# A chunked recurrence inside one decoder block: its small products joined in two stretches a chunk, its decay moved into the next chunk's vectors

## Chip, cores and metric

One core of one Trainium2 chip runs the whole program as one launch. The metric is the device time of that launch in microseconds (us), the median of several runs. The engines are named as in the profile: PE is TensorE (PEld its weight loads), DVE is VectorE, ACT is ScalarE, POOL is GpSimd, SP is SyncE, which here only issues DMAs.

## What is computed

One residual block of a hybrid decoder on 512 tokens of width 1024, all in float32: a norm, one wide input projection, two mixers side by side (a sparse attention and an RWKV-7 recurrence), gates, an output projection, then a gated MLP with a short convolution. The part that matters here is the recurrence: 8 heads, a 64 by 64 state per head, one step for each token.

```python
def step(state, inp):
    r_t, w_t, k_t, v_t, a_t, b_t = inp
    sa = jnp.einsum('bhij,bhj->bhi', state, a_t)
    state = state * w_t[:, :, None, :] + sa[..., None] * b_t[:, :, None, :] + v_t[..., None] * k_t[:, :, None, :]
    return state, jnp.einsum('bhij,bhj->bhi', state, r_t)
...
_, y = lax.scan(step, state0, xs)
...
y = (y - mean) * lax.rsqrt(var + GN_EPS) * ln_g.reshape(H, N) + ln_b.reshape(H, N)
```

`w_t` is the decay, a factor for each channel of the state.

## The kernel before

**The recurrence by chunks.** The 512 tokens are cut into NCH = 8 chunks of C = 64, and the 8 heads stand as 4 pairs (index p) of two (index r). All that does not depend on the state is made ahead of the loop: `AR[:, p, c, 0]` and `AR[:, p, c, 1]` are a chunk's decayed a and r vectors, `BKT` its b and k vectors turned round, `AB` the masked products of these vectors with each other (the part for the state's correction already inverted), `UV` holds the values v and takes up the corrections u, and `PC[:, p, c]` is the decay over the whole of chunk c. The state is the tile `M`, 128 partitions by 256 columns. For chunk c the loop makes these products on PE, each a group of small matrices of 64 by 64:

- X += AR0 · M and Y = AR1 · M, from the state at the chunk's start (32 entries in the trace). X already holds the chunk's own part (`x_own`).
- U = AB · Xs, where `Xs` is X copied to SBUF by DVE, together with `x_own` of the next chunk (32 entries). U is copied into `UV` by ACT and DVE.
- Mp = BKT · UV (16 entries), from which DVE makes the next state in two operations, M1 = (M0 + Mp) * PC, and Y += AB · UV (16 entries), which ACT copies to `Ys`.

Every second chunk `group_norm` normalizes the 128 tokens in `Ys`, on DVE and ACT (`next(gn)`), and then turns them with four transposes on PE beside four small products (`run(gn)`).

**Dense work between them.** These three groups are chained, each waiting for a copy on DVE or ACT of what the one before gave. So the loop calls `next(fill, None)` between them: `fill_chain` is a generator of independent dense work, the rest of the projections and the compression MLP. `dense_fm_g` is one projection of 128 columns, 24 products of 128 by 512 (16 with the high parts `whi`, 8 with the low parts `wlo`), and yields once after the 12th. Weights come by DMA into `raw` (three buffers in turn) from the SP queue; ACT rounds them to `whi`, and DVE (for some POOL) makes `wlo = raw - whi`, one projection ahead.

**What sets the order.** PE and SP take their instructions in the order in which the code writes them (`tc.manual_schedule`). DVE, ACT and POOL are ordered by the framework's scheduler when the program is built, and each then works through its list in order. The products of `kv_proj(1, 280)` and of the compression (`raw,sg` in the trace: 16 products of 128 by 256) come first in the chain. `norm_keys` and `rstd` are short chains on DVE of 8 to 32 columns (`rs_m`, `rs_y`, `kss`, `qss`), after which POOL multiplies the keys and queries (L949, L1008). POOL also issues the DMAs that add up pieces of a later weight (`wsum`).

Of the kernel before, what the change touches and what calls it, by code (L numbers as in the profile page):

```python
# [25 lines left out]
DH = 64  # L26
H = 8
# [56 lines left out]
def hybrid_block(ctx: ExitStack, tc: tile.TileContext, A: dict, out: bass.AP):  # L84
# [28 lines left out]
    def mmb():  # L113
        return bank("mm", 4)

    def pa():
        return bank("a", 2)

    def pb():
        return bank("b", 2)  # L120

    def mm(o, l, r, start, stop):
        te.matmul(o, lhsT=l, rhs=r, start=start, stop=stop)  # L123
# [4 lines left out]
    def act(o, i, f=AF.Copy, **kw):  # L128
        sc.activation(o, i, f, **kw)  # L129

    def tt(o, a, b, op):
        v.tensor_tensor(o, a, b, op=op)  # L132
# [219 lines left out]
    def wsplit_():  # L352
        if loads:
            raw, kt, n, eng = loads.pop(0)
            if eng is None:
                ahead.append(raw)
                return
            if eng == "quarters":
                while len(loads) < len(QUARTER_TILES):
                    wload()  # L360
                ahead.append(first_quarters(raw, *(loads.pop(0)[0] for _ in range(len(QUARTER_TILES) - 1))))
                return
            if type(eng) is tuple:
                eng = eng[1]
                hi, lo = (spare[:, i].rearrange("p (k n) -> p k n", n=n) for i in range(2))
                act(hi, raw)
            else:
                hi = wp.tile([128, kt, n], F32R, name="whi", tag="whi", bufs=2)
                if late:
                    late.pop()(hi, raw)  # L370
                else:
                    act(hi, raw)
                lo = wp.tile([128, kt, n], F32R, name="wlo", tag="wlo", bufs=2)
            ahead.append((hi, lo))
            behind.append(lambda: eng.tensor_tensor(lo, raw, hi.bitcast(F32), op=ALU.subtract))  # L375
            if not hold:
                behind.pop()()

    hold, behind = [], []

    def lows():
        while behind:
# [518 lines left out]
    def heads(ap):  # L901
        return ap.rearrange("p (h d) -> p h d", d=DH)
# [92 lines left out]
    with tc.manual_schedule(engines={mybir.EngineType.PE, mybir.EngineType.Pool, mybir.EngineType.SP}):  # L995
        for m in range(NGA):
            act(siga[m], dense_fm(hh, hl), AF.Tanh, scale=0.5)
        below(0)
        below(16)
        next(fill)  # L1000
        left(0)
        next(fill)
        left(16)
        next(fill)
        norm_keys(0)
        rstd(qss.rearrange("p t h -> p (t h)"), DH)
        for t in range(NT):
            nc.gpsimd.tensor_tensor(heads(qn[:, t]), heads(qn[:, t]), qss[:, t, :, None].to_broadcast([128, 8, DH]),  # L1008
                                    op=ALU.mult)
    dbg("AB", AB)  # L1010
    close(tp_cm)
    kv1 = fill
# [73 lines left out]
        ptv = pt[:, 0:64].rearrange("p (g n) -> p g n", g=2)  # L1086
        act(KC, ptv, AF.Copy, scale=kg)

    def group_norm(c0, Ys):
        n1 = tp.tile([128, H], F32, name="n1", tag="n1", bufs=2)  # L1090
        bc = n1[:, :, None].to_broadcast([128, H, DH])
        v.tensor_reduce(n1, Ys, axis=AX.X, op=ALU.add)
        ts(n1, n1, -1.0 / DH, None)
        tt(Ys, Ys, bc, ALU.add)
        sq = tp.tile([128, H, DH], F32, name="sq", tag="o", bufs=2)
        act(sq, Ys, AF.Square)
        v.tensor_reduce(n1, sq, axis=AX.X, op=ALU.add)
        rstd(n1, DH, 64e-5, "g")
        tt(Ys, Ys, bc, ALU.mult)
        yield  # L1100
        qs = slice(C * c0, C * c0 + 128)
        pt = pa()
        gg = pb()
        o = tp.tile([128, NH2, 128], F32, name="o", tag="o", bufs=2)
        for p in range(NH2):
            ps_ = slice(128 * p, 128 * p + 128)
            te.transpose(pt[:, ps_], Ys[:, 2 * p:2 * p + 2].rearrange("p h d -> p (h d)"), ident)
            mm(gg[:, ps_], g2[:, ps_], sg[:, qs], True, True)
        for p in range(NH2):
            act(o[:, p], pt[:, 128 * p:128 * p + 128], AF.Identity, scale=col("rwkv_ln_g", p),  # L1110
                bias=col("rwkv_ln_b", p))
        tt(o, o, BO[:, :, qs], ALU.add)
        tt(BO[:, :, qs], o, gg.rearrange("p (a t) -> p a t", a=NH2), ALU.mult)
# [26 lines left out]
    def bias_rows(a):  # L1140
        o = 127 - 16 * a
        nc.sync.dma_start(BT[16 * a:16 * a + 16, :, 256:512],
                          vd[:, 0:16 * 384].rearrange("h (i m) -> i h m", m=384)[:, :, o:o + 256])
# [22 lines left out]
    def hsl(r, n=64):  # L1166
        return slice(64 * r, 64 * r + n)
# [8 lines left out]


    with tc.manual_schedule(engines={mybir.EngineType.PE, mybir.EngineType.SP}):
        M0 = Ys = gn = None
        X = pb()  # L1180
        x_own(0, X)
        next(fill, None)
        for c in range(NCH):
            Y = pa()
            if M0 is not None:
                for p in range(NH2):
                    for r in range(2):
                        mm(X[hsl(r), 64 * p:64 * p + 64], AR[hsl(r), p, c, 0, :], M0[hsl(r), p, :], False,
                           p == NH2 - 1)
                    for r in range(2):  # L1190
                        mm(Y[hsl(1 - r), 64 * p:64 * p + 64], AR[hsl(r), p, c, 1, :], M0[hsl(r), p, :], p == 0, False)
            Xs = tp.tile([128, NH2, DH], F32, name="Xs", tag="Xs", bufs=2)
            v.tensor_copy(Xs, X[:, 0:256].rearrange("p (a d) -> p a d", d=DH))
            next(fill, None)
            U = pb()
            if c < NCH - 1:
                X = pb()
            for p in range(NH2):
                for r in range(2):
                    mm(U[hsl(r), 64 * p:64 * p + 64], AB[hsl(r), c, p, r, 0:64], Xs[hsl(r), p], True, True)  # L1200
                if c < NCH - 1:
                    x_own(c + 1, X, (p,))
            act(UV[0:64, c, :, 0, :], U[0:64, 0:256].rearrange("p (a d) -> p a d", d=DH))
            v.tensor_copy(UV[64:128, c, :, 1, :], U[64:128, 0:256].rearrange("p (a d) -> p a d", d=DH))
            next(fill, None)
            if c < NCH - 1:
                Mp = pa()
                for p in range(NH2):
                    for r in range(2):
                        mm(Mp[hsl(r), 64 * p:64 * p + 64], BKT[:, c, p, r, :], UV[:, c, p, r, :], True, True)  # L1210
                M1 = tp.tile([128, NH2, DH], F32, name="M", tag="M", bufs=2)
                mpv = Mp[:, 0:256].rearrange("p (a d) -> p a d", d=DH)
                pc = PC[:, :, c:c + 1].to_broadcast([128, NH2, DH])
                if M0 is None:
                    tt(M1, mpv, pc, ALU.mult)
                else:
                    tt(M1, M0, mpv, ALU.add)
                    tt(M1, M1, pc, ALU.mult)
            for p in range(NH2):
                for r in range(2):  # L1220
                    mm(Y[hsl(1 - r), 64 * p:64 * p + 64], AB[:, c, p, r, 64:128], UV[:, c, p, r, :],
                       M0 is None and p == 0, p == NH2 - 1)
            if c % 2 == 0:
                Ys = tp.tile([128, H, DH], F32, name="Ys", tag="Ys", bufs=2)
            for r in range(2):
                act(Ys[hsl(c % 2), r::2, :], Y[hsl(1 - r), 0:256].rearrange("p (h d) -> p h d", d=DH))
            if c % 2 == 1:
                gn = group_norm(c - 1, Ys)
                if c < NCH - 1:
                    next(gn)  # L1230
            M0 = M1
            if 4 <= c < 6:
                for a in range(4 * c - 16, 4 * c - 12):
                    bias_rows(a)
            if c == NCH - 2:
                bias_compressed()
            if c == NCH - 1:
                for h0 in range(0, H, 4):
                    act(BT[:, h0:h0 + 4, 0:256], BT[:, h0:h0 + 4, 256:257].to_broadcast([128, 4, 256]))
            next(fill, None)  # L1240
            if gn is not None and c % 2 == 0:
                run(gn)
                gn = None
    close(rp_cm)


# [14 lines left out]
    def keys(b):  # L1261
# [7 lines left out]
        for g in range(2):  # L1269
            i, o = slice(64 * g, 64 * g + 64), slice(64 - 64 * g, 128 - 64 * g)  # L1270
            nc.gpsimd.dma_start(KH[o, b, g], KH[i, b, g])
            nc.gpsimd.dma_start(KL[o, b, g], KL[i, b, g])

    def after(inst, other):
        tc.add_manual_dep(inst.ins, other.ins.name, mybir.DependencyInfo(
            mybir.DependencyClass.NoSync, mybir.DependencyReason.DATA), reason="order on one engine")

    def ob_parts(t, behind=None):
        qs = slice(128 * t, 128 * t + 128)
# [786 lines left out]
```

## Time and profile before

| what | value |
|---|---|
| time, median of 3 runs | 790.45 us (790.05 to 791.07) |
| the profiled execution's own time | 790.52 us |
| its span, first to last instruction | 788.8 us |
| PE busy | 782.7 us, 99% of the span |
| DVE busy | 643.1 us, 82% |
| ACT busy | 496.1 us, 63% |
| POOL busy | 110.6 us, 14% |
| the recurrence's loop | about 171 to 270 us of the span |

The span is the time from the first to the last instruction of the profiled execution; 1.7 us of its time lie outside. Busy shares are shares of the span. Products on PE overlap, so a row's duration is longer than the distance to the next row's start; it is the distances between starts that add up.

### The profile page before, as it was taken

The page shows a single profiled execution, that of the slowest core. Times are in us where ns is not written, and L with a number is a line of the kernel's source. Part 1 is how long each engine was busy: PE and PEld are TensorE (multiplying, and loading weights), DVE is VectorE, ACT ScalarE, POOL GpSimd, SP SyncE. Part 2 cuts the span into 40 slices and gives each one's busy share as a digit, 9 for nine tenths or more (in the row PEclk, how much of TensorE's full clock was granted, in tenths as well). Part 3 has the DMA queues.
Part 4 walks back from the last instruction along what each step waited for, and adds up shares of the span by engine and source line. Part 5 has one row for each costly group of instructions (what it writes and reads, how often), then busy time and mean ns, then how long its engine had stood idle before and what let it go on. Part 6 is the DMA issues. An engine that isn't in the chain of part 4 may idle for free.

```text
span 788.8 us, 15333 instructions
## 1 busy us (share of the span) xinstructions
PE 782.7 (99%) x5765; PEld 672.5 (85%) x5765; DVE 643.1 (82%) x1240; ACT 496.1 (63%) x1023; POOL 110.6 (14%) x159
## 2 busy tenths in 40 slices
PE   8999999999999999999999999999999999999998
PEld 7888888987777887777788898899999999888886
DVE  6788889983665588899775489989999999898895
ACT  7977765553444568878335365678888877546452
POOL 6101124141101127111000000110111100000010
PEclk9999999999999999999999999999999999999999
DMA  8456769547877544484268233788888776666821
GB/s 251 110 141 152 177 174 248 143 112 219 204 140 192 127 102 117 113 203 94 69 195 287 92 96 106 195 236 238 205 220 228 209 197 199 222 207 233 272 95 53
DMA packets 149702, 135.52 MB, mean 172 GB/s; under 512 B 7878, under 2 KB 126589, under 8 KB 148733
## 3 DMA queue, kind: packets, MB, share of 16 engines
q1 hardware_dynamic: 139296, 110.10, 46.2%
q0 software_dynamic: 9120, 21.70, 15.7%
q10 hardware_dynamic: 1212, 2.74, 1.1%
q8 instruction: 45, 0.74, 0.4%
q14 instruction: 29, 0.23, 0.1%
HBM read 122.20 MB, written 31.65 MB: 195 GB/s over the span
## 4 chain that ended last, share of the span: by engine, by line
PE 96%; DVE 1%; DMA 1%; ACT 1%; POOL 1%; issue 0%; POOLq 0%; DVEq 0%; ACTq 0%
PE ps_mm L123 55%; PE ps_mm L126 15%; PE ps_a L126 10%; PE ps_a L123 6%; PE ps_b L123 4%; PE ps_b L126 2%; PE ps_b L1501 1%; PE ps_mm L1501 1%; DMA pra<-in_rwkv_ln_b_dram 1%; POOL pra L170 0%; ACT whi L129 0%; DVE wlo L132 0%; PE ps_b L662 0%; PE ps_a L1749 0%; PE ps_a L1255 0%
## 5 line engine op out<-in xcount | busy, mean ns | idle before, releaser
L129 ACT ACTIVATE whi<-raw 128x512 fp32r<-128x512 f32 (+2 forms) x134 | 117.8, 892 | 88.0 <-PE ps_mm L123 40.9
L123 PE MATMUL ps_mm<-hh,whi 128*128 128x512 f32 (+1 forms) x368 | 142.4, 390 | 0.4 <-DVE hl L141 0.4
L123 PE MATMUL ps_mm<-hl,whi 128*128 128x512 f32 (+1 forms) x368 | 139.0, 381 | 0.0
L123 PE MATMUL ps_mm<-hh,wlo 128*128 128x512 f32 (+1 forms) x368 | 89.4, 381 | 0.0
L123 PEld LDWEIGHTS ps_mm<-hh,whi 128*128 128x128 f32 x368 | 69.2, 188 | 15.7 <-DVE hl L141 0.6
L123 PEld LDWEIGHTS ps_mm<-hl,whi 128*128 128x128 f32 x368 | 69.3, 188 | 12.2
L123 PEld LDWEIGHTS ps_mm<-hh,wlo 128*128 128x128 f32 x368 | 67.1, 188 | 13.6
L302 POOL DMA_DIRECT2D wsum<-in_w_up_dram x48 | 38.9, 869 | 229.9 <-DMA wsum<-wsum 141.8
L375 DVE TENSOR_TENSOR wlo<-raw,whi 128x1024 fp32r<-128x1024 f32 (+1 forms) x51 | 53.6, 1052 | 20.8 <-PE ps_mm L123 10.7
L132 DVE TENSOR_TENSOR wlo<-raw,whi 128x512 fp32r<-128x512 f32 (+1 forms) x64 | 58.5, 934 | 9.7 <-ACT whi L129 7.6
L141 DVE SCALAR_TENSOR_TENSOR right<-ps_mm,cw,right 128x511 f32<-128x511 f32 (+1 forms) x64 | 45.3, 740 | 0.9 <-ACT right L129 0.8
L336 POOL DMA_DIRECT2D right<-right x16 | 13.9, 869 | 206.8 <-DVE right L132 97.3
L129 ACT ACTIVATE P<-P,nm 128x512 f32<-128x512 f32 (+3 forms) x64 | 35.3, 553 | 5.9 <-DVE nm L1427 5.1
L126 PE MATMUL ps_mm<-hh,whi 128*128 128x256 f32 x128 | 32.1, 283 | 0.0
L126 PE MATMUL ps_mm<-hl,whi 128*128 128x256 f32 x128 | 32.1, 283 | 0.0
L1427 DVE CUSTOM_DVE_ANT_0 P<-ps_a,AB 128x512 f32<-128x512 f32 (+3 forms) x64 | 29.1, 485 | 3.2 <-PE ps_a L123 2.8
L129 ACT ACTIVATE QK<-ps_mm 128x64 f32<-128x64 f32 (+5 forms) x56 | 14.8, 309 | 18.1 <-PE ps_mm L123 18.0
L129 ACT ACTIVATE right<-ps_mm,cw 128x512 f32<-128x512 f32 x32 | 23.9, 769 | 3.0 <-DVE ps_mm L141 1.9
L126 PEld LDWEIGHTS ps_mm<-hh,whi 128*128 128x128 f32 x128 | 24.6, 192 | 0.0
L126 PEld LDWEIGHTS ps_mm<-hl,whi 128*128 128x128 f32 x128 | 24.6, 192 | 0.0
L123 PE MATMUL ps_mm<-whi,hh 128*128 128x280 f32 (+2 forms) x72 | 22.5, 333 | 0.0
L129 ACT ACTIVATE whi<-T 128x1024 fp32r<-128x1024 f32 (+1 forms) x12 | 11.9, 989 | 16.2 <-DVE T L132 7.6
(499 smaller groups left out, 2131.2 us busy)
## 6 DMA issues: line engine op xcount, KB each, us to landing
raw<-in_w_in_dram SPq DMA_DIRECT2D x38, 512.0 KB, 5.2
wsum<-in_w_up_dram POOLq DMA_DIRECT2D x48, 256.0 KB, 5.3
raw<-in_w_down_dram SPq DMA_DIRECT2D x18, 512.0 KB, 3.9
wsum<-wsum SPq DMA_DIRECT2D x32, 256.0 KB, 5.1
right<-in_w_up_dram SPq DMA_DIRECT2D x32, 256.0 KB, 4.1
raw<-wsum SPq DMA_DIRECT2D x32, 256.0 KB, 3.6
raw<-in_w_up_dram SPq DMA_DIRECT2D x32, 256.0 KB, 4.2
raw<-in_w_up_dram SPq DMA_DIRECT2D x12, 512.0 KB, 4.9
```

Source lines behind the costliest of these rows:

```text
L123: te.matmul(o, lhsT=l, rhs=r, start=start, stop=stop)
L126: te.matmul(o, lhsT=l, rhs=r, start=False, stop=stop, skip_group_check=True)
L129: sc.activation(o, i, f, **kw)
L132: v.tensor_tensor(o, a, b, op=op)
L141: v.scalar_tensor_tensor(o, a, s, b, op0=op0, op1=op1)
L302: nc.gpsimd.dma_start(o, x, accum_op=ALU.add)
L336: nc.gpsimd.dma_start(raw[:, 4:8], raw[:, 0:4], accum_op=ALU.add)
L375: behind.append(lambda: eng.tensor_tensor(lo, raw, hi.bitcast(F32), op=ALU.subtract))
L1427: maxima.append(v.tensor_tensor_reduce(out=P[:, i], in0=o, in1=BT[:, h, 384 - 128 * qt:512], scale=-1.0, scalar=-NEG, op0=ALU.add, op1=ALU ...
L1501: te.transpose(pt[:, 128 * i:128 * i + 128], P[:, 4 * x + i, 128 * k:128 * k + 128], ident)
```

## The change

In the loop over chunks, the products of a chunk that end it (BKT · UV for the state, AB · UV for the outputs) now stand at the head of the next pass, right ahead of the products with the new state. A pass has two stretches of small products: BKT · UV, AB · UV and AR · M of the new chunk in one, U in the other. The new functions `state`, `outputs` and `finished` hold what was written out in the loop before. The dense step that stood between AB · UV and AR · M now follows the one ahead of BKT · UV, so two dense steps stand together.

- `state` puts BKT · UV into two banks (pairs 0 and 1 in one, 2 and 3 in the other) and adds each half to the state with an operation of its own, or copies it in the first chunk. The multiplication by PC is no part of it any more.
- The decay is applied in two other places: POOL multiplies the next chunk's `AR` by PC, once a chunk (128 by 512), and DVE makes M0 = M1 * PC, which only the next addition reads.
- `after` (moved up unchanged) fixes an order on one engine: POOL's multiplications of AR stand behind those of the queries (`roots`), and a DVE `wlo` behind the last addition to the state that was written before it (`states`).
- `group_norm` takes its two banks from the dense ring in the loop; its products now stand ahead of U. The bias loads (`bias_rows`, `bias_compressed`) and ACT's broadcast into `BT` come one chunk later in the code.

```diff
@@ -372,11 +372,20 @@
                     act(hi, raw)
                 lo = wp.tile([128, kt, n], F32R, name="wlo", tag="wlo", bufs=2)
             ahead.append((hi, lo))
-            behind.append(lambda: eng.tensor_tensor(lo, raw, hi.bitcast(F32), op=ALU.subtract))
+            def low():
+                inst = eng.tensor_tensor(lo, raw, hi.bitcast(F32), op=ALU.subtract)
+                if states and eng is v:
+                    after(inst, states[-1])
+
+            behind.append(low)
             if not hold:
                 behind.pop()()
 
-    hold, behind = [], []
+    hold, behind, states = [], [], []
+
+    def after(inst, other):
+        tc.add_manual_dep(inst.ins, other.ins.name, mybir.DependencyInfo(
+            mybir.DependencyClass.NoSync, mybir.DependencyReason.DATA), reason="order on one engine")
 
     def lows():
         while behind:
@@ -1005,8 +1014,8 @@
         norm_keys(0)
         rstd(qss.rearrange("p t h -> p (t h)"), DH)
         for t in range(NT):
-            nc.gpsimd.tensor_tensor(heads(qn[:, t]), heads(qn[:, t]), qss[:, t, :, None].to_broadcast([128, 8, DH]),
-                                    op=ALU.mult)
+            roots = nc.gpsimd.tensor_tensor(heads(qn[:, t]), heads(qn[:, t]),
+                                            qss[:, t, :, None].to_broadcast([128, 8, DH]), op=ALU.mult)
     dbg("AB", AB)
     close(tp_cm)
     kv1 = fill
@@ -1086,7 +1095,7 @@
         ptv = pt[:, 0:64].rearrange("p (g n) -> p g n", g=2)
         act(KC, ptv, AF.Copy, scale=kg)
 
-    def group_norm(c0, Ys):
+    def group_norm(c0, Ys, dense_banks=False):
         n1 = tp.tile([128, H], F32, name="n1", tag="n1", bufs=2)
         bc = n1[:, :, None].to_broadcast([128, H, DH])
         v.tensor_reduce(n1, Ys, axis=AX.X, op=ALU.add)
@@ -1099,8 +1108,7 @@
         tt(Ys, Ys, bc, ALU.mult)
         yield
         qs = slice(C * c0, C * c0 + 128)
-        pt = pa()
-        gg = pb()
+        pt, gg = (mmb(), mmb()) if dense_banks else (pa(), pb())
         o = tp.tile([128, NH2, 128], F32, name="o", tag="o", bufs=2)
         for p in range(NH2):
             ps_ = slice(128 * p, 128 * p + 128)
@@ -1176,22 +1184,74 @@
 
 
     with tc.manual_schedule(engines={mybir.EngineType.PE, mybir.EngineType.SP}):
-        M0 = Ys = gn = None
+        M0 = Ys = Y = gn = None
+
+        def state(c):
+            Mps = [pb(), mmb()]
+            for p in range(NH2):
+                for r in range(2):
+                    mm(Mps[p // 2][hsl(r), 64 * p:64 * p + 64], BKT[:, c, p, r, :], UV[:, c, p, r, :], True, True)
+            M1 = tp.tile([128, NH2, DH], F32, name="M", tag="M", bufs=2)
+            for i, ps in enumerate(Mps):
+                ps_ = slice(2 * i, 2 * i + 2)
+                o = ps[:, 128 * i:128 * i + 128].rearrange("p (a d) -> p a d", d=DH)
+                if M0 is None:
+                    last = v.tensor_copy(M1[:, ps_], o)
+                else:
+                    last = v.tensor_tensor(M1[:, ps_], M0[:, ps_], o, op=ALU.add)
+            states[:] = [last]
+            return M1
+
+        def outputs(c, Y):
+            for p in range(NH2):
+                for r in range(2):
+                    mm(Y[hsl(1 - r), 64 * p:64 * p + 64], AB[:, c, p, r, 64:128], UV[:, c, p, r, :],
+                       c == 0 and p == 0, p == NH2 - 1)
+
+        def finished(c, Y, Ys):
+            for r in range(2):
+                act(Ys[hsl(c % 2), r::2, :], Y[hsl(1 - r), 0:256].rearrange("p (h d) -> p h d", d=DH))
+
         X = pb()
         x_own(0, X)
         next(fill, None)
         for c in range(NCH):
+            before = Y
+            if c:
+                M1 = state(c - 1)
+                outputs(c - 1, before)
             Y = pa()
-            if M0 is not None:
+            if c:
                 for p in range(NH2):
                     for r in range(2):
-                        mm(X[hsl(r), 64 * p:64 * p + 64], AR[hsl(r), p, c, 0, :], M0[hsl(r), p, :], False,
+                        mm(X[hsl(r), 64 * p:64 * p + 64], AR[hsl(r), p, c, 0, :], M1[hsl(r), p, :], False,
                            p == NH2 - 1)
                     for r in range(2):
-                        mm(Y[hsl(1 - r), 64 * p:64 * p + 64], AR[hsl(r), p, c, 1, :], M0[hsl(r), p, :], p == 0, False)
+                        mm(Y[hsl(1 - r), 64 * p:64 * p + 64], AR[hsl(r), p, c, 1, :], M1[hsl(r), p, :], p == 0, False)
             Xs = tp.tile([128, NH2, DH], F32, name="Xs", tag="Xs", bufs=2)
             v.tensor_copy(Xs, X[:, 0:256].rearrange("p (a d) -> p a d", d=DH))
+            if c:
+                if c % 2 == 1:
+                    Ys = tp.tile([128, H, DH], F32, name="Ys", tag="Ys", bufs=2)
+                finished(c - 1, before, Ys)
+                if c % 2 == 0:
+                    gn = group_norm(c - 2, Ys, True)
+                    next(gn)
+                if c < NCH - 1:
+                    M0 = tp.tile([128, NH2, DH], F32, name="M0", tag="M0", bufs=1)
+                    tt(M0, M1, PC[:, :, c - 1:c].to_broadcast([128, NH2, DH]), ALU.mult)
+            if c < NCH - 1:
+                a_ = AR[:, :, c + 1].rearrange("p a r t -> p a (r t)")
+                after(nc.gpsimd.tensor_tensor(a_, a_, PC[:, :, c:c + 1].to_broadcast([128, NH2, 2 * C]), op=ALU.mult), roots)
+            if 5 <= c < 7:
+                for a in range(4 * c - 20, 4 * c - 16):
+                    bias_rows(a)
+            if c == NCH - 1:
+                bias_compressed()
             next(fill, None)
+            if gn is not None and c % 2 == 1:
+                run(gn)
+                gn = None
             U = pb()
             if c < NCH - 1:
                 X = pb()
@@ -1204,43 +1264,14 @@
             v.tensor_copy(UV[64:128, c, :, 1, :], U[64:128, 0:256].rearrange("p (a d) -> p a d", d=DH))
             next(fill, None)
             if c < NCH - 1:
-                Mp = pa()
-                for p in range(NH2):
-                    for r in range(2):
-                        mm(Mp[hsl(r), 64 * p:64 * p + 64], BKT[:, c, p, r, :], UV[:, c, p, r, :], True, True)
-                M1 = tp.tile([128, NH2, DH], F32, name="M", tag="M", bufs=2)
-                mpv = Mp[:, 0:256].rearrange("p (a d) -> p a d", d=DH)
-                pc = PC[:, :, c:c + 1].to_broadcast([128, NH2, DH])
-                if M0 is None:
-                    tt(M1, mpv, pc, ALU.mult)
-                else:
-                    tt(M1, M0, mpv, ALU.add)
-                    tt(M1, M1, pc, ALU.mult)
-            for p in range(NH2):
-                for r in range(2):
-                    mm(Y[hsl(1 - r), 64 * p:64 * p + 64], AB[:, c, p, r, 64:128], UV[:, c, p, r, :],
-                       M0 is None and p == 0, p == NH2 - 1)
-            if c % 2 == 0:
-                Ys = tp.tile([128, H, DH], F32, name="Ys", tag="Ys", bufs=2)
-            for r in range(2):
-                act(Ys[hsl(c % 2), r::2, :], Y[hsl(1 - r), 0:256].rearrange("p (h d) -> p h d", d=DH))
-            if c % 2 == 1:
-                gn = group_norm(c - 1, Ys)
-                if c < NCH - 1:
-                    next(gn)
-            M0 = M1
-            if 4 <= c < 6:
-                for a in range(4 * c - 16, 4 * c - 12):
-                    bias_rows(a)
-            if c == NCH - 2:
-                bias_compressed()
-            if c == NCH - 1:
-                for h0 in range(0, H, 4):
-                    act(BT[:, h0:h0 + 4, 0:256], BT[:, h0:h0 + 4, 256:257].to_broadcast([128, 4, 256]))
-            next(fill, None)
-            if gn is not None and c % 2 == 0:
-                run(gn)
-                gn = None
+                next(fill, None)
+        outputs(NCH - 1, Y)
+        finished(NCH - 1, Y, Ys)
+        states.clear()
+        gn = group_norm(NCH - 2, Ys)
+        for h0 in range(0, H, 4):
+            act(BT[:, h0:h0 + 4, 0:256], BT[:, h0:h0 + 4, 256:257].to_broadcast([128, 4, 256]))
+        next(fill, None)
     close(rp_cm)
```

POOL's list, from the `wlo` ahead of the keys on. Before:

```order
L949 TENSOR_TENSOR QK<-QK,kss 128x128 x4
L1008 TENSOR_TENSOR QK<-QK,qss 128x512 x4
L949 TENSOR_TENSOR QK<-QK,kss 128x128 x4
L302 DMA wsum_102<-in_w_up_dram 64x1024 x2
L302 DMA wsum_103<-in_w_up_dram 64x1024 x8
```

And now (keys, queries, then `AR` times `PC`):

```order
L958 TENSOR_TENSOR QK<-QK,kss 128x128 x4
L1017 TENSOR_TENSOR QK<-QK,qss 128x512 x4
L1245 TENSOR_TENSOR AR<-AR,PC 128x4x128 x7
L958 TENSOR_TENSOR QK<-QK,kss 128x128 x4
L302 DMA wsum_102<-in_w_up_dram 64x1024 x2
L302 DMA wsum_103<-in_w_up_dram 64x1024 x8
```

All seven multiplications stand in a row between the queries and the second group of keys; no DMA stands among them.

DVE's list at the first state, from the copy of the first chunk's u into `UV` on. Before:

```order
L1204 COPY UV<-ps_b 64x4x64
L132 TENSOR_TENSOR M<-ps_a,PC 128x256
L375 TENSOR_TENSOR wlo<-raw,whi 128x1024
L138 TENSOR_SCALAR rs_m<-kss 128x8
L138 TENSOR_SCALAR kss<-rs_m 128x8
L138 TENSOR_SCALAR gts<-gts 128x96
L132 TENSOR_TENSOR rs_y<-kss 128x8
```

And now, from the last round of that same chain on `kss` on (M_2265 is the tile M0):

```order
L132 TENSOR_TENSOR rs_y<-kss 128x8
L141 SCALAR_TENSOR_TENSOR rs_y<-rs_y,rs_m 128x8
L141 SCALAR_TENSOR_TENSOR kss<-rs_y,kss 128x8
L1199 COPY M<-ps_b 128x128
L1199 COPY M<-ps_mm 128x128
L132 TENSOR_TENSOR M_2265<-M,PC 128x256
L1232 COPY Xs<-ps_b 128x256
```

The first state was made ahead of that `wlo` and of the chain of `norm_keys(1)`; now both stand ahead of it. They are the same operations as before: the `wlo`, the scaling of `gts`, and eleven of 8 columns.

PE's list at the same place. Before:

```order
L123 MATMUL ps_mm<-wlo,hh 128x280 x5
L123 MATMUL ps_a<-UV,BKT 64x64 x8
L123 MATMUL ps_a<-UV,AB 64x64 x8
L123 MATMUL ps_mm<-raw,sg_1740 64x256 x8
L123 MATMUL ps_mm<-hh,whi 128x512
```

And now, from the twelfth product of the dense step that follows `raw,sg` on:

```order
L123 MATMUL ps_mm<-hl,whi 128x512
L123 MATMUL ps_b<-UV,BKT 64x64 x4
L123 MATMUL ps_mm<-UV,BKT 64x64 x4
L123 MATMUL ps_a<-UV,AB 64x64 x8
L123 MATMUL ps_b<-M,AR 64x64 x2
L123 MATMUL ps_a<-M,AR 64x64 x2
```

BKT · UV and AB · UV have moved behind `raw,sg` and twelve dense products, and AR · M follows them with nothing between.

## Rows read from the trace of the kernel before

**Rows 1.** Page, first part: busy us, share of the span, instructions

```profile
PE 782.7 (99%) x5765; PEld 672.5 (85%) x5765; DVE 643.1 (82%) x1240; ACT 496.1 (63%) x1023; POOL 110.6 (14%) x159
```

**Rows 2.** Waits of PE, whole span: us in total, times, longest us

```profile
PE ps_b L123 <- DVE warm L156: 1.2, 1, 1.2
```

**Rows 3.** Timeline of PE at chunk 1's AR · M: start, us, instruction, count

```profile
185.96 0.39 PE L123 MATMUL ps_mm<-hl,whi 128*128 128x512 f32 x1
186.28 0.27 PE L123 MATMUL ps_b<-M,AR 64*64 64x64 f32 x2
...
186.39 0.23 PE L123 MATMUL ps_b<-M,AR 64*64 64x64 f32 x2
...
186.44 0.22 PE L123 MATMUL ps_b<-M,AR 64*64 64x64 f32 x2
...
186.74 0.23 PE L123 MATMUL ps_b<-M,AR 64*64 64x64 f32 x2
...
186.91 0.50 PE L123 MATMUL ps_mm<-hh,whi 128*128 128x512 f32 x1
187.24 0.39 PE L123 MATMUL ps_mm<-hl,whi 128*128 128x512 f32 x1
187.47 0.40 PE L123 MATMUL ps_mm<-hh,whi 128*128 128x512 f32 x1
```

**Rows 4.** Timeline of PE where AR · M of chunk 4 meets other small products

```profile
225.52 0.22 PE L123 MATMUL ps_b<-M,AR 64*64 64x64 f32 x2
...
225.69 0.92 PE L123 MATMUL ps_mm<-QK 128*32 128x64 f32 x24
```

**Rows 5.** Timeline of PE at the end of chunk 0

```profile
180.48 0.69 PE L123 MATMUL ps_a<-UV,BKT 128*64 128x64 f32 x16
181.00 0.64 PE L123 MATMUL ps_a<-UV,AB 128*64 128x64 f32 x16
181.47 1.90 PE L123 MATMUL ps_mm<-raw,sg 128*64 128x256 f32 x16
183.29 0.50 PE L123 MATMUL ps_mm<-hh,whi 128*128 128x512 f32 x1
```

**Rows 6.** Timeline of ACT at the same place

```profile
181.49 1.06 ACT L129 ACTIVATE whi<-raw 128x1024 fp32r<-128x1024 f32 x1 [2.04 <-DMA raw<-in_w_in_dram]
```

**Rows 7.** Timeline of DVE from there to chunk 1's Xs

```profile
182.58 1.23 DVE L375 TENSOR_TENSOR wlo<-raw,whi 128x1024 fp32r<-128x1024 f32 x1 [0.94 <-ACT whi L129]
183.84 0.17 DVE L138 TENSOR_SCALAR rs_m<-kss 128x8 f32<-128x8 f32 x1
...
186.06 0.17 DVE L141 SCALAR_TENSOR_TENSOR kss<-rs_y,kss 128x8 f32<-128x8 f32 x1
187.01 0.43 DVE L1193 COPY Xs<-ps_b 128x256 f32<-128x256 f32 x1 [0.79 <-PE ps_b L123]
```

**Rows 8.** Timeline of POOL, 170 to 200 us: its multiplications there

```profile
175.84 4.05 POOL L1008 TENSOR_TENSOR QK<-QK,qss 128x512 f32<-128x512 f32 x4
186.37 1.48 POOL L949 TENSOR_TENSOR QK<-QK,kss 128x128 f32<-128x128 f32 x4 [6.47 <-DVE kss L141]
```

**Rows 9.** Timelines of POOL and DVE where both work from SBUF at once

```profile
167.71 1.15 DVE L132 TENSOR_TENSOR sg<-QK,prm 128x248 f32<-128x248 f32 x2
168.35 1.70 POOL L375 TENSOR_TENSOR wlo<-raw,whi 128x560 fp32r<-128x560 f32 x1 [4.42 <-ACT AB L129]
168.76 1.70 DVE L132 TENSOR_TENSOR sg<-QK,prm 128x248 f32<-128x248 f32 x1
...
15.74 2.42 POOL L375 TENSOR_TENSOR wlo<-raw,whi 128x1024 fp32r<-128x1024 f32 x1
...
17.60 0.59 DVE L136 TENSOR_SCALAR w0h<-prm 128x4 f32<-128x4 f32 x1
```

**Rows 10.** The program's end: PE's last row; window with PE's granted clock after POOL

```profile
784.77 0.40 PE L123 MATMUL ps_b<-wlo,Sb 128*128 128x256 f32 x2
...
788.00:788.80 0.80, 0.00 (x0) 0.00 (x0) 0.00 (x0) 0.00 (x0) 0.00 (x0) 0.85 0.00 0
```

More of the change, by code (lines that the diff above doesn't have):

```diff
@@ L1272, in keys @@
             nc.gpsimd.dma_start(KL[o, b, g], KL[i, b, g])
-    def after(inst, other):
-        tc.add_manual_dep(inst.ins, other.ins.name, mybir.DependencyInfo(
-            mybir.DependencyClass.NoSync, mybir.DependencyReason.DATA), reason="order on one engine")
     def ob_parts(t, behind=None):
```

## The prediction

> **What bounds the kernel now.** The first part of the page comes first: PE is busy 99% of the span, DVE 82% [rows 1]. Then the waits of PE: the longest in the whole program is 1.2 us, at its start [rows 2], and in the loop it waits for nobody. So a change here is worth what it takes from PE's own list, less any wait that it puts into it. Nothing later gives such a wait back, since PE stays the bound to the end. A wait of 0.2 us on PE is 0.2 us of the time.
>
> **What joining saves.** I read PE's starts, not its durations. Inside dense work a product starts 0.23 us after the one before (187.24 to 187.47). Where dense work meets small products three of these distances grow [rows 3]. The last dense product holds the first small one for 0.32 us (185.96 to 186.28), 0.09 more than 0.23. The first small pair takes 0.11 (186.28 to 186.39) where the next take 0.05 to 0.06. The last small pair holds the dense one for 0.17 (186.74 to 186.91), 0.11 more than 0.06, and the first dense product takes 0.33 (186.91 to 187.24), 0.10 more. Together 0.35 us for a stretch.
>
> Joining two dense steps takes away the 0.09 and the 0.10: 0.19 us. Whether it also takes away the other two, 0.16, depends on how AB · UV (tiles of 128 by 64) passes to AR · M (64 by 64). No row shows this pair. The nearest is AR · M followed by small products of another shape: 0.17 (225.52 to 225.69), just what it pays before a dense product [rows 4]. So I take 0.19 for a joint, and keep 0.35 as its upper bound.
>
> [...]
>
> There are seven joints, at chunks 1 to 7. At chunk 5 the two transposes of the compression fall between the two dense steps, so nothing is joined there; chunk 1 I walk through below. Five are left: 5 x 0.19 = 0.95 us.
>
> **Chunk 1, step by step.** Before, BKT · UV and AB · UV ran from 180.48 to 181.47, 0.99 us; `raw,sg` followed, and the dense step began at 183.29 [rows 5]. Without that stretch PE is at the dense step at 183.29 - 0.99 = 182.30. Its weights are not there: ACT's rounding began at 181.49, when the DMA had landed, and took 1.06 [rows 6], so they come at 182.55. That cover, 0.74 us before, is gone: **a wait of 0.25**. The twelve dense products took 183.29 to 186.28, 2.99 us, with the step to small products [rows 3, 5]; so the joined stretch begins at 185.54. BKT and AB take 0.99, and 0.11 for the switch: AR · M is due at 186.64.
>
> It needs the first state. DVE used to make this ahead of the `wlo` and of the chain on `kss`; now it stands behind both. Alone they would be in time: the `wlo` starts at 182.58, the chain runs from 183.84 to 186.23 (the last row's 186.06 + 0.17), 2.39 us [rows 7]. The two copies of 128 columns have no row; they lie between nothing and the 0.43 of `Xs` with 256 [rows 7], and I take 0.28. The first half would be there at 186.51.
>
> But DVE is not alone any more. POOL's four multiplications of the queries take 4.05 us, 1.01 each, and end at 179.90 [rows 8]; seven on `AR` of the same size follow at once, to 186.98 by the same price. The trace shows what happens when both engines read two operands from SBUF. A DVE product of 248 columns takes 0.57 (two in 1.15); the one issued at 168.76, while POOL worked from 168.35 to 170.05, took 1.70, until 0.41 after POOL was done [rows 9]. POOL's own row, 560 columns, took 1.70 too, where 1024 alone took 2.42, that is 1.32 for 560: it had first waited for DVE. So they take turns, a whole instruction each, and the one that waits is served ahead of the next of the other. Even 4 columns of a `tensor_scalar` took 0.59, until POOL's row of 15.74 + 2.42 = 18.16 was over, against 0.17 for the 8 columns of `rs_m` [rows 7, 9].
>
> [...]
>
> So from 182.58 on the port works off, one after the other: what is left of POOL's seven, 186.98 - 182.58 = 4.40; the `wlo`, 1.23; the chain, 2.39. Sum 8.02: whoever goes first, the chain ends at about 190.60 while a multiplication of `AR` slips in between any two of its operations. The copy adds 0.28: AR · M starts at 190.88 instead of 186.64, **a wait of 4.24**. The bounds: if only the `wlo` is held, for the rest of POOL's third multiplication (179.90 + 3.03 = 182.93), the chain ends at 182.93 + 1.23 + 2.39 = 186.55, the copy at 186.83, and the wait is 0.19. If `AR`, which lies in four pieces, costs as much as POOL's `wlo` (2.42 for 1024, 1.21 for 512) instead of 1.01, the seven take 1.4 longer and the wait is 5.6.
>
> From there AR · M takes its 0.63 [rows 3] and ends at 191.51; before, it ended at 186.91. That is 4.60 late.
>
> **What else is moved, at nothing.** The products are the same in number. M0 = M1 * PC stays on DVE where the multiplication by PC was, off the path now; the addition in two halves hides behind AB · UV, half a microsecond of PE. The later chunks' `AR` is long done: chunk 2 needs it some 12 us on. POOL's second group of keys comes later by about 4 us, for transposes at the end of the loop. The weight DMA behind a slot that PE frees comes earlier by the stretch taken away; the others follow PE.
>
> **Sum.** 790.52 (the profiled execution, 0.07 over the median) + 4.60 - 0.95 = 794.17, so **794.2 us**. The likeliest case's own range, from a joint's bounds (0.8 less) and from those of `AR` (1.4 more), is 793.3 to 795.6.
>
> **Rivals.**
>
> - *POOL holds up the `wlo` and not the chain.* For it: the chain's rows are of 8 columns, and no row shows one beside POOL. Against it: the 4 columns that took 0.59. The place is the same; it decides from where the chain ends before 186.4. Then the wait is 0.19 in place of 4.24: 794.17 - 4.05 = **790.1**, no change.
> - *The same, and no switch inside the stretch.* 5 x 0.16 less, and the 0.11 at chunk 1: **789.2**, and with whi's wait gone too 789.0. Rows 4 speak against it. A little more, and it is faster.
> - *The pause lowers PE's clock.* PE's last product ends at 785.17 (784.77 + 0.40), and the granted clock is still full until 788; the window from 788.0 to 788.8 shows a mean of 0.85, so it fell there, after about 3 us of nothing to do [rows 10]. [...] I take 1.8: **796.0**.
>
> [...]
>
> **Chances.** The port held for the whole chain 0.55 (794.2); that and the clock 0.13 (796.0); the chain not held 0.20 (790.1); that without the switch 0.07 (789.2); 0.05 for a wait that I don't see. A measurement here can tell 0.2%, 1.6 us: slower begins at 792.0, faster ends at 788.9. The first two cases and part of the last give slower 0.72; the third and most of the fourth give same 0.21; faster 0.07. The range, 789.7 to 796.3, holds the first three cases, with the clock's price up to about 2 us; it leaves out the fourth and what lies beyond.
>
> **What would show it.** In PE's waits one of about 4 us for DVE at the first AR · M, which begins near 190.9; 0.25 for ACT's whi ahead of it. On DVE the chain's rows near 184 to 190 with durations of about 1 us in place of 0.17, POOL's `AR` rows between them, some longer than 1.0. From chunk 2 on each joined stretch 0.19 shorter than its parts. The forecast is wrong if those rows keep 0.17: then the time is about 790.

## The result, and the profile after

| what | before | after |
|---|---|---|
| median, 6 runs each | 790.32 us (790.05 to 791.07) | 795.22 us (792.60 to 795.73) |
| ratio, 95% interval | | 1.0056 (1.0042 to 1.0070) |
| profiled execution, its span | 790.52, 788.8 us | 795.34, 793.6 us |

The change makes the kernel 0.6% slower. Five of the six executions took 794.7 to 795.7 us at a mean granted clock of 0.995 to 0.997; one took 792.6, and its clock was full. That difference is explained below.

The page's first part, beside [rows 1], has nearly the same busy time on PE, 8 us more on POOL and 3 on DVE:

```profile
PE 782.8 (99%) x5765; PEld 673.6 (85%) x5765; DVE 646.3 (81%) x1247; ACT 496.3 (63%) x1023; POOL 118.8 (15%) x166
```

The waits of PE, beside [rows 2]: engine, tile and line waited for, us in total, times, longest.

```profile
PE ps_b L123 <- DVE M L1199: 3.3, 1, 3.3
PE ps_mm L448 <- DVE rx_y L433: 1.3, 1, 1.3
...
PE ps_mm L123 <- ACT whi L129: 0.2, 1, 0.2
```

The second row is the program's start and costs nothing here: the products that wait for `rx_y` start at 7.57 us, the same ones at 7.51 before the change, and at chunk 0 the two kernels are level (177.73 and 177.72).

The timeline of PE at chunk 1, which answers to [rows 3] and [rows 5]:

```profile
180.49 1.95 PE L123 MATMUL ps_mm<-raw,sg 128*64 128x256 f32 x16
182.61 0.50 PE L123 MATMUL ps_mm<-hh,whi 128*128 128x512 f32 x1 [0.17 <-ACT whi L129]
...
185.56 0.45 PE L123 MATMUL ps_b<-UV,BKT 128*64 128x64 f32 x8
185.84 0.40 PE L123 MATMUL ps_mm<-UV,BKT 128*64 128x64 f32 x8
186.07 0.64 PE L123 MATMUL ps_a<-UV,AB 128*64 128x64 f32 x16
189.97 0.37 PE L123 MATMUL ps_b<-M,AR 64*64 64x64 f32 x2 [3.26 <-DVE M L1199]
...
191.03 0.79 PE L123 MATMUL ps_mm<-hh,whi 128*128 128x512 f32 x1
191.62 0.63 PE L123 MATMUL ps_mm<-hl,whi 128*128 128x512 f32 x1
```

PE has 3.26 us of nothing to do, and what comes after it is slow: the dense products stand 0.43 us apart (191.62, 192.05, 192.48) where they stood 0.23 apart. The windows of the same stretch say why; behind the length of the window stand the busy times of PE, PEld, DVE, ACT and POOL, and behind these PE's granted clock:

```profile
187.00:188.00 1.00, 0.00 (x0) 0.00 (x0) 0.97 (x2) 0.52 (x2) 1.00 (x2) 1.00 1.11 316
188.00:189.00 1.00, 0.00 (x0) 0.00 (x0) 0.83 (x6) 0.00 (x0) 0.07 (x1) 0.83 1.08 279
189.00:190.00 1.00, 0.03 (x4) 0.06 (x5) 0.90 (x5) 0.00 (x0) 0.36 (x1) 0.50 1.07 329
190.00:192.00 2.00, 2.00 (x34) 1.74 (x35) 1.31 (x4) 1.06 (x1) 1.30 (x4) 0.50 0.56 152
192.00:195.00 3.00, 3.00 (x8) 2.31 (x7) 0.98 (x1) 0.00 (x0) 0.00 (x0) 0.50 0.00 0
195.00:196.00 1.00, 1.00 (x4) 0.53 (x2) 0.00 (x0) 0.00 (x0) 0.00 (x0) 0.76 0.00 0
196.00:198.00 2.00, 2.00 (x45) 1.47 (x46) 0.43 (x1) 0.97 (x2) 0.00 (x0) 1.00 0.00 0
```

In the pause the granted clock falls from 1.00 to 0.50, and it is full again only from the window that begins at 196. What PE waits for is in the timelines of DVE and POOL, beside [rows 7] and [rows 8]:

```profile
182.59 1.51 DVE L376 TENSOR_TENSOR wlo<-raw,whi 128x1024 fp32r<-128x1024 f32 x1 [2.76 <-ACT whi L129]
184.03 1.01 DVE L138 TENSOR_SCALAR rs_m<-kss 128x8 f32<-128x8 f32 x1
184.96 0.20 DVE L138 TENSOR_SCALAR gts<-gts 128x96 f32<-128x96 f32 x1
185.08 1.01 DVE L138 TENSOR_SCALAR kss<-rs_m 128x8 int32<-128x8 int32 x1
186.13 0.97 DVE L132 TENSOR_TENSOR rs_y<-kss 128x8 f32<-128x8 f32 x1
187.13 0.97 DVE L141 SCALAR_TENSOR_TENSOR rs_y<-rs_y,rs_m 128x8 f32<-128x8 f32 x1
188.13 0.17 DVE L141 SCALAR_TENSOR_TENSOR kss<-rs_y,kss 128x8 f32<-128x8 f32 x1
...
189.33 0.17 DVE L141 SCALAR_TENSOR_TENSOR kss<-rs_y,kss 128x8 f32<-128x8 f32 x1
189.53 0.29 DVE L1199 COPY M<-ps_b 128x128 f32<-128x128 f32 x1
189.74 0.28 DVE L1199 COPY M<-ps_mm 128x128 f32<-128x128 f32 x1
...
179.97 8.10 POOL L1245 TENSOR_TENSOR AR<-AR,PC 128x512 f32<-128x512 f32 x7
```

While POOL works, to 179.97 + 8.10 = 188.07, four operations on 8 columns take about 1 us each; after it they take 0.17. The copies of the first state stand behind the last of them.

**Where the 4.8 us lie.** The first `Xs,AB` product of each chunk is a mark in PE's list. Its start, in us:

| chunk | 0 | 1 | 2 | 3 | 4 | 5 | 6 | 7 |
|---|---|---|---|---|---|---|---|---|
| before | 177.72 | 189.85 | 204.79 | 217.29 | 229.48 | 242.25 | 253.42 | 265.93 |
| after | 177.73 | 196.04 | 210.73 | 223.03 | 234.99 | 247.75 | 258.72 | 271.02 |
| later by | 0.01 | 6.19 | 5.94 | 5.74 | 5.51 | 5.50 | 5.30 | 5.09 |

Chunk 1 loses 6.2 us. Chunks 2, 3, 4, 6 and 7 give back 0.25, 0.20, 0.23, 0.20 and 0.21; chunk 5, where two transposes stand between the dense steps, gives 0.01. PE's last product is 4.81 late.

### The profile page after: what moved, and what is told of

It reads as the page before. It is cut to its first block, busy times and chain, and to the rows that moved or that the text cites. A ratio compares the mean times of both kernels' runs of the same rounds, so it can differ in the third digit from the quotient of the medians.

```text
span 793.6 us, 15359 instructions
## 1 busy us (share of the span) xinstructions
PE 782.8 (99%) x5765; PEld 673.6 (85%) x5765; DVE 646.3 (81%) x1247; ACT 496.3 (63%) x1023; POOL 118.8 (15%) x166
## 4 chain that ended last, share of the span: by engine, by line
PE 95%; DVE 2%; DMA 1%; ACT 1%; POOL 0%; issue 0%; SPq 0%; POOLq 0%; ACTq 0%; DVEq 0%
PE ps_mm L123 54%; PE ps_mm L126 15%; PE ps_a L126 10%; PE ps_a L123 6%; PE ps_b L123 4%; PE ps_b L126 2%; PE ps_b L1528 1%; PE ps_mm L1528 1%; DMA raw<-in_w_in_dram 1%; DMA pra<-in_rwkv_ln_b_dram 1%; ACT whi L129 1%; POOL pra L170 0%; DVE wlo L132 0%; PE ps_b L671 0%; PE ps_a L1776 0%
```

## The experiments

Theory A is the prediction's: POOL's multiplications and DVE's operations block each other, so POOL stretches the chain on `kss`, and the first state stands behind that chain. Theory B: the chain delays the state by standing ahead of it, whatever POOL does. Theory C: the wait for `whi` and the joining itself cost the time.

| run | median us (lowest to highest, runs) | ratio to before, 95% |
|---|---|---|
| e1_one_ahead | 789.72 (789.31 to 790.70, 11) | 0.9992 (0.9983 to 1.0001) |
| e2_act_copies | 789.75 (789.41 to 790.20, 11) | 0.9990 (0.9981 to 0.9999) |
| e3_state_first | 789.69 (789.34 to 790.18, 11) | 0.9990 (0.9981 to 0.9999) |
| e4_filled | 798.03 (797.73 to 798.86, 4) | 1.0095 (1.0082 to 1.0109) |
| e5_before_load | 790.36 (790.10 to 791.31, 11) | 0.9998 (0.9989 to 1.0007) |
| e6_decay_on_dve | 789.56 (789.32 to 790.00, 11) | 0.9988 (0.9979 to 0.9997) |
| e7_five_ahead | 791.16 (791.04 to 791.43, 11) | 1.0010 (1.0001 to 1.0018) |
| e8_six_ahead | 792.32 (791.90 to 795.01, 11) | 1.0029 (1.0020 to 1.0038) |
| e9_filled_y | 793.24 (792.95 to 794.43, 5) | 1.0036 (1.0022 to 1.0050) |

**One multiplication ahead (e1).** `keyed` holds POOL's last multiplication of the second keys.

```diff
-                after(nc.gpsimd.tensor_tensor(a_, a_, PC[...], op=ALU.mult), roots)
+                after(nc.gpsimd.tensor_tensor(a_, a_, PC[...], op=ALU.mult),
+                      roots if c < 1 else keyed[-1])
```

> The changed kernel, but only chunk 1's multiplication of AR follows the queries on POOL; the other six stand behind the second keys. DVE's list is unchanged: the chain on kss still stands ahead of the two copies of the first state. Theory A (POOL and DVE take turns at a shared port, so POOL's seven multiplications stretch the wlo and the chain): POOL's one multiplication is over near 181, before the wlo begins at 182.6; wlo 1.2 us, chain operations 0.17 each, copies near 186.3, PE's wait at AR x M at most 0.2 in place of 3.26, granted clock full there. Time: the profiled changed kernel is 4.8 us over the one before; at chunk 1's U it stands 6.18 behind, of which 3.26 are the wait and 2.5 the half clock; 0.42 stays, and the later joints give 1.38 back. 790.5 + 0.42 - 1.38 = 789.6. Theory B (the list order alone: the chain stands ahead of the copies, whatever POOL does): wait of 2 us or more, 793 to 795. Theory C (what costs is the wait for whi and the joining itself): no change, 795.

Measured 789.72. DVE's rows, with the chain where it was in DVE's list, and PE's:

```profile
184.00 0.17 DVE L138 TENSOR_SCALAR rs_m<-kss 128x8 f32<-128x8 f32 x1
...
186.04 0.17 DVE L141 SCALAR_TENSOR_TENSOR kss<-rs_y,kss 128x8 f32<-128x8 f32 x1
186.33 0.29 DVE L1201 COPY M<-ps_b 128x128 f32<-128x128 f32 x1
...
186.91 0.27 PE L123 MATMUL ps_b<-M,AR 64*64 64x64 f32 x2
```

POOL's one multiplication ends at 181.22; with POOL silent behind it the chain is through at 186.2, and PE doesn't wait for the state. B and C are out: the order and the joints are those of the changed kernel. The profiled execution ran 0.28 late already at chunk 0 (178.01); from there chunk 1's mark (190.50) comes 0.36 later than before, the price of the lost cover for `whi` and of the passage inside the stretch.

**The same load on the kernel before (e5).** The product is not by the decay: in the columns used here the tile `ones` holds 1 in the first 64 partitions and 0 in the other 64, so the output is another, for the same amount of work (8.05 us on POOL).

```diff
+        for c in range(1, NCH):
+            a_ = AR[:, :, c].rearrange("p a r t -> p a (r t)")
+            nc.gpsimd.tensor_tensor(a_, a_, ones[:, 0:4, None].to_broadcast([128, NH2, 2 * C]), op=ALU.mult)
```

> The kernel before, with seven POOL multiplications of AR's chunks by ones right behind the queries: the same load on the port, and no other part of the change. Theory A: the wlo takes about 1.5 us and the chain's first operations about 1 us each, to 189.5 in place of 186.2, as in the changed kernel, but the first state is made ahead of both, so PE waits for nothing at AR x M; Xs of chunk 1 stands behind the chain and comes at 189.9, when PE wants it (189.85): 0 to 0.3. 790.5 to 790.9, no change. A theory by which the chain's stretching needs something else of the change (its other order, the copies) keeps the chain's rows at 0.17. One by which the load on POOL costs time by itself: 793 or more.

Measured 790.36, no change, and the stretched rows are there:

```profile
181.87 0.42 DVE L132 TENSOR_TENSOR M<-ps_a,PC 128x256 f32<-128x256 f32 x1 [1.39 <-PE ps_a L123]
183.24 1.43 DVE L375 TENSOR_TENSOR wlo<-raw,whi 128x1024 fp32r<-128x1024 f32 x1 [0.95 <-ACT whi L129]
184.59 1.00 DVE L138 TENSOR_SCALAR rs_m<-kss 128x8 f32<-128x8 f32 x1
185.62 0.97 DVE L138 TENSOR_SCALAR kss<-rs_m 128x8 int32<-128x8 int32 x1
```

POOL's load alone stretches the chain and costs nothing, since the state is made ahead of it. It takes both: the load, and the state behind the chain.

**The state out of the chain's way (e2, e3).** In e2 ACT copies the first state. In e3 the call `norm_keys(1)` stands behind the first state's products in the code, and its first operation is ordered behind the state's copies on DVE. POOL keeps all seven.

```diff
-                    last = v.tensor_copy(M1[:, ps_], o)
+                    act(M1[:, ps_], o)
...
-            states[:] = [last]
+            states[:] = [last] if M0 is not None else []
```

```diff
+        first = v.tensor_scalar(m, ap, 1.0 / n, eps, op0=ALU.mult, op1=ALU.add)
+        if states:
+            after(first, states[-1])
...
+                if c == 1:
+                    norm_keys(1)
```

> The changed kernel with the two copies of the first state made by ACT in place of DVE; POOL's seven multiplications stay where they are. Theory A: the chain on DVE is stretched as before, to 189.5, but the state no longer stands behind it; ACT is idle from 183.8 and copies at 186.1 to 186.7, so AR x M waits 0 to 0.3. Xs stands behind the chain and M0 x PC on DVE, 189.5 + 0.6 + 0.4 = 190.6, and PE wants it at 190.4: up to 0.3 more. 789.6 to 790.2; 789.9. Theory B gives the same. Theory C: 795. A theory by which copies out of PSUM are held by POOL's port as well, on whatever engine, keeps a wait near 3 us: 793 to 795.

> The changed kernel with the norm of the second keys ordered behind the first state's copies on DVE; POOL's seven multiplications stay where they are. Theory A: wlo 1.5 us as now, copies at 186.1 to 186.7 from PSUM, AR x M waits 0 to 0.3; the chain is held until POOL is done at 188.1 and runs on past 189; Xs stands among its operations and comes near 189.5 to 190, PE wants it at 190.4. 789.6 to 790.2. If a copy from PSUM is held for one of POOL's multiplications, 0.5 to 1.0 more: 790.7. Theory C: 795.

Measured 789.75 and 789.69. In e2 the chain's first operations still take 0.97 to 1.01, and the state that ACT copies is in time: AR · M starts at 186.93, 0.57 behind AB · UV, and PE has no wait for it. In e3, with POOL at work from 180.00 to 188.34:

```profile
184.06 1.05 DVE L138 TENSOR_SCALAR gts<-gts 128x96 f32<-128x96 f32 x1
186.09 0.29 DVE L1198 COPY M<-ps_b 128x128 f32<-128x128 f32 x1 [0.97 <-PE ps_b L123]
186.32 0.29 DVE L1198 COPY M<-ps_mm 128x128 f32<-128x128 f32 x1
186.53 0.57 DVE L185 TENSOR_SCALAR rs_m<-kss 128x8 f32<-128x8 f32 x1
187.01 0.41 DVE L132 TENSOR_TENSOR M<-M,PC 128x256 f32<-128x256 f32 x1
187.34 1.02 DVE L138 TENSOR_SCALAR kss<-rs_m 128x8 int32<-128x8 int32 x1
```

The copies read PSUM, and POOL does not hold them: 0.29 each. `gts`, a `tensor_scalar` that reads SBUF and took 0.21 before the change, is held: 1.05. The prediction had no row of a copy from PSUM beside POOL.

**Decay on DVE, nothing on POOL (e6).**

```diff
...
+                        last = v.scalar_tensor_tensor(M1[:, p], o, pc, M0[:, p], op0=ALU.mult, op1=ALU.add)
...
-                after(nc.gpsimd.tensor_tensor(a_, a_, PC[:, :, c:c + 1].to_broadcast([128, NH2, 2 * C]), op=ALU.mult), roots)
```

> The changed kernel without POOL's seven multiplications: AR stays unscaled, and DVE multiplies by the decay as it takes the products out of PSUM, in four instructions of 64 columns (scale and add in one) in place of two of 128; stretches joined as in the change, the chain still ahead of the state. Theory A: with nothing on POOL the chain's rows are 0.17 and it ends at 186.2; four instructions of about 0.2 each end at 187.0, AR x M takes them piece by piece, so it waits 0.1 to 0.3 at chunk 1, and 0 to 0.2 at each later chunk if four take longer than two did: 789.6 to 790.8; 789.9. Theory B (the list order alone): a wait of 2 us or more as in the changed kernel, 793 to 795.

Measured 789.56: without POOL's multiplications, and with twice as many instructions for the state, PE waits for no state. It says the same as e1.

**Five and six ahead (e7, e8).** As e1, with `c < 5` and `c < 6`.

> The changed kernel with five of POOL's seven multiplications behind the queries and two behind the second keys. Theory A: each multiplication less lets one operation of the chain go in 0.2 in place of 1.0; POOL is done near 186.1, the chain at 187.9 in place of 189.5, AR x M at 188.4 in place of 189.97: a wait of 1.7. Without a fall of the clock 789.7 + 1.7 = 791.4; if so short a pause lowers it as well, 2.5 more, 793.9. Theory B: 795. The run also shows whether the clock needs the whole pause of 3.3.

> The changed kernel with six of POOL's seven multiplications behind the queries and one behind the second keys. Theory A: POOL done near 187.1, the chain at 188.7, AR x M at 189.2: a wait of 2.5. Without a fall of the clock 789.7 + 2.5 = 792.2; with it 794.7. Theory B: 795.

The waits of PE, of e7 and of e8:

```profile
PE ps_b L123 <- DVE M L1201: 1.6, 1, 1.6
```

```profile
PE ps_b L123 <- DVE M L1201: 2.2, 1, 2.2
```

The wait shrinks with the number of multiplications ahead of the second keys: 3.26 with seven, 2.25 with six, 1.59 with five, none with one. e7 has a full clock (0.999 or 1.000) in all 11 runs. In e8 six runs have it and took 791.9 to 792.3; five have 0.995 to 0.998 and took 793.3 to 795.0. So with a pause of 2.25 us the clock fell in some executions of one kernel, with one of 1.6 in none here; the pause itself is measured only in the one execution of each kernel that was profiled.

**The pause filled (e4, e9).** 28 products that nobody reads, ahead of chunk 1's AR · M; in e4 into a bank of the state's products, in e9 into Y.

```diff
+            for _ in range(28 if c == 1 else 0):
+                mm(Y[:, 256:512], hh[:, 0, 0:128], hh[:, 0, 0:256], True, True)
```

> The changed kernel with 28 products of 256 columns on PE, of operands that are there anyway and into columns that nobody reads, between AB x UV and AR x M of chunk 1 (in the dense work 512 columns take 0.23, so these take about 28 x 0.115 = 3.2 us). The wait for the first state stays, since DVE and POOL are untouched: AR x M starts near 190.0. The pause is filled, nothing else is taken away. If it is the pause that lowers the granted clock, the clock stays full and the 2.5 us that the half clock cost after 190 come back: 795.2 - 2.5 = 792.7. If the clock falls there for another reason, or the loss behind 190 is not the clock's, 795.2 stays.

> The changed kernel with 28 products of 256 columns between AB x UV and AR x M of chunk 1, now into columns of chunk 1's own bank Y that nobody reads, so that they wait for nobody: from 186.7 to about 189.9 PE has work. DVE and POOL are untouched, AR x M still starts near 190.0. If the pause lowers the granted clock, it stays full now and the 2.5 us lost at half clock come back: 795.2 - 2.5 = 792.7, in every execution. If the clock falls for another reason: 795.2.

e4 missed: 798.03. Its products write the bank that DVE's copy reads, so they stood behind the copy, and the pause stayed:

```profile
189.99 6.14 PE L123 MATMUL ps_mm<-hh 128*128 128x256 f32 x28 [3.32 <-DVE M L1201]
196.06 0.27 PE L123 MATMUL ps_b<-M,AR 64*64 64x64 f32 x2
```

They took 6.07 us, at a granted clock of 0.50 to 195 and a mean of 0.63 in the window from 195 to 196. All four executions have a granted clock of 0.995 to 0.998. In e9 the products run in the pause, in 3.55:

```profile
186.63 3.62 PE L123 MATMUL ps_a<-hh 128*128 128x256 f32 x28
190.18 0.27 PE L123 MATMUL ps_b<-M,AR 64*64 64x64 f32 x2
```

```profile
189.00:190.00 1.00, 1.00 (x11) 1.00 (x9) 0.88 (x5) 0.00 (x0) 0.40 (x2) 1.00 1.06 316
...
191.00:192.00 1.00, 1.00 (x5) 0.83 (x5) 0.00 (x0) 0.89 (x1) 0.25 (x1) 1.00 0.13 35
```

The state comes as late as ever, AR · M even 0.2 later, yet the kernel is 2.0 us faster, with the granted clock at 0.999 or 1.000 in all five runs. So here it is the pause that lowers the clock, and about 2.2 us of the loss (the 2.0 and the 0.2) are the clock's.

## Why the prediction was right, and where it was not

Forecast: 794.2 us, slower at 0.72. Measured: 795.2, inside the range and slower. The mechanism was the one named. Two terms of the sum were mis-sized, in opposite directions: the chain's end came 1.1 us earlier, and the clock cost 2.5 us where the likeliest case had nothing. So the nearness of the two times is partly luck.

| step | forecast | measured |
|---|---|---|
| joined stretch begins | 185.54 | 185.56 |
| AR · M due | 186.64 | 186.64 (1.08 behind BKT, as in e1) |
| chain ends | 190.60 | 189.50 |
| AR · M starts | 190.88 | 189.97 |
| AR · M late at full clock | 4.60 | 3.69 (189.97 against 186.28) |
| the clock | 0 | 2.50 |
| five joints | -0.95 | -1.09 |

*The wait for `whi`* was put at 0.25; the row has 0.17, and by starts the dense step is 0.30 late (182.61 against 180.49 + 1.82). Right.

*The port*, the prediction's name for what POOL and DVE take turns at, is right in kind. No row shows a port; what the rows show is the waiting: e1 and e5 show POOL's load as the cause of the stretched rows. The size was wrong by 1.1 us at the chain's end, and by 0.9 at AR · M, which starts 0.47 behind that end (189.97 against 189.50) where 0.28 was taken. The step that failed is the sum 4.40 + 1.23 + 2.39, which gives the whole chain time of its own on the port. Its first operations cost POOL nothing: seven multiplications and a `wlo` between them took 8.10, that is 7.07 by the price of 1.01 and 1.03 for the `wlo`. Each held operation waited out one multiplication and went by at its end: the four end at 185.04, 186.09, 187.10 and 188.10, POOL's next multiplications start at 184.98, 186.03 and 187.03, and its last ends at 188.07. So the chain ends at POOL's end, 188.07, plus the seven operations that are left, 7 x 0.20 = 1.40: 189.5, as in the trace. The same sum gives e7 and e8: POOL done near 186.0 with nine left, 187.8; near 187.0 with eight left, 188.6. The rows end at 187.79 and 188.62. The prediction speaks of two operands read from SBUF, but two of the four held operations, `rs_m` and the first `kss`, read only one; for these its row of 4 columns [rows 9] was the better ground.

*The clock* was a rival, with a chance of 0.13 and a price of 1.8 us, the author's estimate, which no run shows. The clock fell in five of six executions; in the profiled one that cost 2.5 us in place of 1.8: AR · M and the step behind it took 189.97 to 191.03, 0.43 more than 0.63, and the dense work to the next mark 5.01 in place of 2.94, 2.07 more. The step that failed is the likeliest case's silence on it. It leaned on [rows 10], where the clock fell after about 3 us of nothing (a mean of 0.85 in the last window); e8 shows it falling in five of eleven executions with a pause of 2.25, and the changed kernel's trace to 0.50 from 189 on, in a wait of 3.26.

*The joints* were put at 0.19, with nothing at chunk 5: measured 0.20 to 0.25, and 0.01 there. The passage inside the stretch is paid, as taken: AB · UV to AR · M at chunk 2 is 204.72 to 205.28, 0.56; before, AB · UV to the dense product there was 195.82 to 196.39, 0.57.

*The sum.* 790.52 + 3.69 + 2.50 - 1.10 (chunks 2 to 7) = 795.61; 795.34 was measured. The remaining 0.3 is won back between 378 and 382 us of the span before the change, in a stretch of small products with `PTs,Vr`: PE is 5.12 late ahead of it and 4.81 behind it. Why is open, and the spread of one kernel's runs is larger. The likeliest case, the port with a full clock, is the one execution at 792.6, and e9; by the measured terms it is 790.52 + 3.69 - 1.10 = 793.1. That 794.2 lies within 1.0 us of the median is owed to two errors that go against each other, -0.9 at AR · M and +2.5.

*POOL holds up the `wlo` alone*, the rival at 790.1, is refuted by the rows of 1.0 us; *no switch* by the joints.

With the stall gone (e1, e2, e3, e6) the rest of the change is worth 0.8 us, 0.1%: near what can be told from no change. Five joints give 1.1, and chunk 1 costs 0.36.

## What to carry to other kernels

Work moved to an idle engine is not free if it holds up the engine that makes the next thing PE waits for (795.2 us here with seven multiplications on POOL, 789.6 with none): look at which engine is at work at the same time, and what stands ahead of the critical instruction in its list. Here each member of a chain of small dependent operations on DVE waited out about one of POOL's instructions (1.0 us in place of 0.17) as long as POOL was at work, so this chain was a bad thing to put ahead of a critical copy. The pause on PE cost its length and, in five of six executions, clock behind it (0.50 granted in the profiled one): the step from a wait of 1.6 us to one of 3.3 cost 4.1 us.

## What the runs showed of the hardware that was not expected

- Copies from PSUM passed POOL's multiplications unhindered (0.29 each in e3), and so did a product with one operand in PSUM (0.42 in e5, and 0.42 before the change with POOL silent), while an operation on 8 columns from SBUF took 0.96 to 1.00 there in place of 0.17.
- An independent instruction behind a held one passed with it: `gts` took 0.20 right behind the held `rs_m` (after) or the held `kss` (e5), but 1.05 where it was the first in line (e3). So did even the product of two operands in SBUF, M0 = M1 * PC with 256 columns: 0.41 behind `rs_m` in e3, with POOL at work.
- The clock's fall is a matter of the execution, not of the kernel alone: none of eleven runs with a pause of 1.6 us (e7), five of eleven with 2.25 (e8), five of six with 3.3 (the changed kernel), each pause as measured in one execution.
- At a granted clock of 0.50 both dense and small products took about twice their distance (0.43 for 0.23, 0.11 for 0.06), with PE busy without a gap from 189.97 until the clock was back (a mean of 0.76 from 195 to 196, 1.00 from 196 on).
